# A fixed TensorE order for the scan stage of mixer groups 1 to 3, with the y products of two chunks in a row

## The chip, the cores and the metric

The kernel runs on one core of a Trainium2 chip. The metric is the device time of one execution in microseconds (us): 1355.12, the median of three runs (1355.06 to 1355.35). Five engines work side by side, each with its own in-order queue of instructions: TensorE (PE; its weight loads are shown apart as PEld), VectorE (DVE), ScalarE (ACT), GpSimd (POOL) and SyncE (SP, which here issues weight transfers). They wait for one another through semaphores.

## The reference

The reference is a two-layer decoder trunk on 512 tokens with a width of 1024. Layer 0 is a Mamba-2 mixer and a gated feed-forward block with a short convolution; layer 1 is a differential attention and the same kind of feed-forward block. The change lies in the mixer. It projects the normed input to a gate z, to x, B and C (which pass a causal convolution of width 4 and a SiLU) and to a step dt. Then it runs a chunked scan, in 4 groups of 8 heads, over chunks of 128 tokens:

```
cb       = einsum('bclgn,bcsgn->bcgls', cc, bc)
y_diag   = einsum('bcgls,bgrcls,bcsgrp->bclgrp', cb, decay_in, xc)
states   = einsum('bclgn,bgrcl,bclgrp->bcgrpn', bc, decay_states, xc)
new_states = einsum('bgrzc,bcgrpn->bzgrpn', decay_chunk, states0)
y_off    = einsum('bclgn,bcgrpn,bgrcl->bclgrp', cc, states_in, exp(a_cs))
y        = (y_diag + y_off + x * d_skip) * silu(z)
```

Then y is normed within its group and projected back, and the result is added to the residual stream.

## The kernel before

Every large product is made of three matmuls on split operands: weights high times input high, weights high times input low, weights low times input high (`mm3`, L195 to L198). One such set of three on a block of 128 of the contraction is called a triple here. A weight chunk is fetched by SyncE, its high part is copied by ScalarE (`wh`, L147), and VectorE subtracts to get the low part (`wl`, L151). `chunk()` (L187) emits these two chunks ahead of use, in the order of the list `plan`.

The mixer loops over four groups (L755). For each group the program does the following, in this order:

1. It fetches the decay masks of the four chunks through GpSimd's DMA queue (`fetch`, L618: `m`, four buffers, and `er`, two buffers).
2. It makes six convolution blocks (`conv_block`, L526): one for B (`bT`), one for C (`cT`), four for x (`xs`). Each is 24 matmuls into a `ps_in` bank, a multiplication, three shifted multiply-adds (`ctmp`, L534) and a SiLU. The norm of the group before (`normed`, L738) lies between the first two.
3. It runs the scan of the group's four chunks and the four z blocks (`z_blocks`, L710). A z block is eight triples, or 24 matmuls, into a `ps_in` bank, then a multiplication by the norm's factor (L714) and a SiLU (L715).
4. It multiplies y by z (L777), sums squares (`gsq`, `gacc`) and makes the norm's factor (`token_rsqrt`, with the transposes `tr_g`).
5. It projects the group before (`out_proj`, L698, `ps_o`). In group 3 the norm's factor and the norm are made inside the projection of group 2, and group 3's own projection follows at once.

The scan of a chunk (class `Chunk`, L606) has these steps. `tokens` (L647) transposes the chunk's x (`xs`, four transposes) and scales it by dt (`xd`, VectorE) and by the decay (`xe`, VectorE); for all but the last chunk it also transposes B (`bt` into a bank, then ScalarE copies it out, L661). `masked` (L639) multiplies C and B (`cb`, L643) and VectorE multiplies the decay mask `m` by it (L644). `states` (L663) first makes the part of y that comes from the state before (`yo`, L669, with VectorE's multiplication into `er`, L671), then the chunk's state (`st`, L674) and from it the running state `S` (ScalarE for chunk 0, two VectorE operations later). `outputs` (L682) makes the diagonal part of y: eight calls (`y`, L689), two of them side by side on the two halves of the array's columns, since each has 64 output rows; VectorE then adds the skip term and the state's part in place (L693, L696). The profile records `cb`, `yo`, `st` and `y` with two records for a call, a transpose with one.

Each of these small products takes one of four PSUM banks (`aux_bank`, L60); z and the projections take one of four others (`mm_bank`).

What sets the order: a planner takes the instructions of the program, and with its own costs and the order in which the program names them as priority, it lays out the queue of each engine before the kernel runs. Before the change the program names a step of the scan and z blocks in turn (`weave`, L470), and the planner mixes scan products and z triples on TensorE as it sees operands become ready. Some stretches are fixed by hand: inside `tc.manual_schedule` TensorE keeps the order of the program, as the attention does already (L1133).

Of the kernel before, what the change touches and what calls it, by code (L numbers as in the profile page):

```python
# [9 lines left out]
F32 = mybir.dt.float32  # L10
F32R = mybir.dt.float32r
I32 = mybir.dt.int32
AF = mybir.ActivationFunctionType
ALU = mybir.AluOpType
# [4 lines left out]
P = 128  # L19
T = 512  # L20
D = 1024
KB = D // P
NT = T // P
# [16 lines left out]
def trunk_kernel(ctx: ExitStack, tc, x, ssm_ln_g, ssm_in_w, ssm_conv_w, ssm_conv_b, ssm_dt_bias,  # L40
# [4 lines left out]
    act, dve, pool, pe, sync = nc.scalar, nc.vector, nc.gpsimd, nc.tensor, nc.sync  # L45
# [11 lines left out]
    def mm_bank(name):  # L57
        return pp.tile([P, T], F32, tag="mm", name=name)

    def aux_bank(name):  # L60
        return pp.tile([P, T], F32, tag="aux", name=name)
# [62 lines left out]
    state = {"next": 0, "use": 0}  # L124
# [62 lines left out]
    def chunk(key):  # L187
        while state["next"] <= state["use"] + AHEAD and state["next"] < len(plan):
            emit_chunk()
        state["use"] += 1  # L190
        k, h, l = ready.pop(0)
        assert k == key, (k, key)
        return h, l

    def mm3(ps, wh, wl, xh, xl, start, stop):  # L195
        pe.matmul(ps, wh, xh, start=start, stop=False)  # L196
        pe.matmul(ps, wh, xl, start=False, stop=False)  # L197
        return pe.matmul(ps, wl, xh, start=False, stop=stop).ins  # L198
# [4 lines left out]
    ident = cp.tile([P, P], F32, name="ident")  # L203
# [13 lines left out]
    xgh = [gp.tile([P, T], F32R, name="xgh%d" % k) for k in range(KB)]  # L217
    xgl = [gp.tile([P, T], F32R, name="xgl%d" % k) for k in range(KB)]
# [19 lines left out]
    with tc.tile_pool(name="ph0", bufs=1) as p0:  # L238
# [24 lines left out]
        ps = aux_bank("pst")  # L263
# [206 lines left out]
    def weave(main, fill, num, den):  # L470

        owed = 0
        for _ in main:
            owed += num
            while owed >= den:
                owed -= den
                next(fill, None)
        run(fill)
# [37 lines left out]
    with tc.tile_pool(name="ssm_y", bufs=1) as yp, tc.tile_pool(name="ssm", bufs=1) as sp:  # L516
# [89 lines left out]
        class Chunk:  # L606
# [40 lines left out]
            def tokens(self):  # L647

                tag, cs = self.tag, self.cs
                ps = aux_bank("xs" + tag)  # L650
                for b in range(4):
                    pe.transpose(ps[:, b * P:(b + 1) * P], self.xs[:, b, cs], ident)
                self.xd = sp.tile([P, HPG, 64], F32, tag="xd", name="xd" + tag, bufs=2)
                dve.tensor_tensor(out=self.xd, in0=byh(ps), in1=self.per_head(dt), op=ALU.mult)
                if self.c < NT - 1:
                    self.xe = sp.tile([P, HPG, 64], F32, tag="xe", name="xe" + tag, bufs=2)
                    dve.tensor_tensor(out=self.xe, in0=self.xd, in1=self.per_head(dl), op=ALU.mult)
                    ps = aux_bank("bt" + tag)
                    pe.transpose(ps[:, :P], self.bT[:, cs], ident)
                    self.bt = sp.tile([P, P], F32, tag="bt", name="bt" + tag, bufs=2)  # L660
                    act.activation(self.bt, ps[:, :P], AF.Copy)  # L661

            def states(self):  # L663

                tag, c = self.tag, self.c
                if c:
                    ps = aux_bank("yo" + tag)
                    for b in range(4):
                        pe.matmul(ps[:, b * P:(b + 1) * P], fl(self.prev.S[:, 2 * b:2 * b + 2, :]),  # L669
                                  self.cT[:, self.cs], start=True, stop=True)  # L670
                    dve.tensor_tensor(out=fl(self.er), in0=ps, in1=fl(self.er), op=ALU.mult)  # L671
                if c < NT - 1:
                    ps = aux_bank("st" + tag)
                    pe.matmul(ps, self.bt, fl(self.xe), start=True, stop=True)  # L674
                    self.S = sp.tile([P, HPG, 64], F32, tag="S", name="S" + tag, bufs=2)
                    if c == 0:
                        act.activation(fl(self.S), ps, AF.Copy)
                    else:
                        dve.tensor_tensor(out=self.S, in0=self.prev.S, in1=self.per_head(et), op=ALU.mult)
                        dve.tensor_tensor(out=self.S, in0=byh(ps), in1=self.S, op=ALU.add)  # L680

            def outputs(self):  # L682

                g, c, cs = self.g, self.c, self.cs
                ps = aux_bank("y" + self.tag)
                for b in range(4):
                    o = ps[:, b * P:(b + 1) * P]
                    for j in range(2):
                        pe.matmul(o[64 * j:64 * (j + 1), :], self.xd[:, 2 * b + j, :], self.m[:, 4 * j + b, :],  # L689
                                  start=True, stop=True)  # L690
                for b in range(4):
                    x_ = self.xs[:, b, cs]
                    dve.scalar_tensor_tensor(out=x_, in0=x_, scalar=c2[:, 64 + 4 * g + b:65 + 4 * g + b],  # L693
                                             in1=ps[:, b * P:(b + 1) * P], op0=ALU.mult, op1=ALU.add)
                if c:
                    dve.tensor_tensor(out=self.xs[:, :, cs], in0=self.xs[:, :, cs], in1=self.er, op=ALU.add)  # L696
# [13 lines left out]
        def z_blocks(g, zs):  # L710
            for b in range(4):
                ps = in_block("in%d" % (4 * g + b))
                z = sp.tile([P, T], F32, tag="z", name="z%d_%d" % (g, b), bufs=4)
                dve.tensor_tensor(out=z, in0=ps, in1=rr[0], op=ALU.mult)  # L714
                act.activation(z, z, AF.Silu)  # L715
                zs.append(z)
                yield

        def chunks(g, bT, cT, xs):
            cs = []  # L720
            for c in range(NT):
                cs.append(Chunk(g, c, bT, cT, xs, cs[-1] if cs else None))
            return cs

        def scan(cs):
            for t in range(NT + 1):
                if t < NT:
                    cs[t].tokens()
                    cs[t].masked()
                if t == 0:  # L730
                    cs[2].decays()
                    cs[3].decays()
                if t:
                    cs[t - 1].states()
                    cs[t - 1].outputs()
                yield

        def normed(g, xs, rt):  # L738
            with tc.issue_after(state["last"]):
# [15 lines left out]
        for g in range(NG):  # L755
            bT = sp.tile([P, T], F32, tag="bT", name="bT%d" % g, bufs=2)
            cT = sp.tile([P, T], F32, tag="cT", name="cT%d" % g, bufs=2)
            xs_ = sp.tile([P, 4, T], F32, tag="xs", name="xs%d" % g, bufs=2)
            cs = chunks(g, bT, cT, xs_)
            for c in cs:  # L760
                c.fetch()
            conv_block(16 + g, "in%d" % (32 + g), bT)
            if g:
                prev = normed(*todo)
            conv_block(20 + g, "in%d" % (36 + g), cT)
            if g == 0:
                params_a()
            xs = [xs_[:, b, :] for b in range(4)]
            for b in range(4):
                if b >= 2:  # L770
                    cs[b - 2].decays()
                conv_block(4 * g + b, "in%d" % (16 + 4 * g + b), xs[b])
            zs = []
            weave(scan(cs), z_blocks(g, zs), 2, 3)
            acc = None
            for b in range(4):
                dve.tensor_tensor(out=xs[b], in0=xs[b], in1=zs[b], op=ALU.mult)  # L777
                sq = sp.tile([P, T], F32, tag="gsq", name="gsq%d_%d" % (g, b), bufs=2)
                act.activation(sq, xs[b], AF.Square)
                if b == 0:  # L780
                    acc = sq
                else:
                    a2 = sp.tile([P, T], F32, tag="gacc", name="gacc%d_%d" % (g, b), bufs=2)
                    (pool if b == 1 else dve).tensor_tensor(out=a2, in0=acc, in1=sq, op=ALU.add)
                    acc = a2
            factor = lambda: token_rsqrt(acc, sp, "g%d" % g, 512)
            if g == 0:
                params_b()
                todo = g, xs, factor()
            elif g < NG - 1:  # L790
                run(out_proj(g - 1, *prev, None))
                todo = g, xs, factor()
            else:
                op = out_proj(g - 1, *prev, None)
                for _ in range(3):
                    next(op)
                rt = factor()
                for _ in range(2):
                    next(op)
                prev = normed(g, xs, rt)  # L800
                run(op)
# [406 lines left out]
```

## Time and profile before

| | us |
|---|---|
| median of three runs | 1355.12 |
| lowest and highest | 1355.06, 1355.35 |
| the profiled execution | 1354.9 |
| its span, first to last instruction | 1353.2 |
| scan stage of group 1, from its first transpose to the projection's first matmul | 121.42 to 156.98 |
| scan stage of group 2 | 212.33 to 247.74 |
| scan stage of group 3 | 303.09 to 338.54 |

The times of the stages are starts in the timeline, from the span's start. A record of a matmul is longer than the distance between two matmuls, since they are pipelined: a matmul of 512 columns is recorded with 0.39 us, and the next starts 0.23 us later. So distances are taken from end to end (start plus length), or from the chain of work that ended last, which counts each piece from the end of the piece before it.

### The profile page before, as it was taken

The page shows a single profiled execution, that of the slowest core. Times are in us where ns is not written, and L with a number is a line of the kernel's source. Part 1 is how long each engine was busy: PE and PEld are TensorE (multiplying, and loading weights), DVE is VectorE, ACT ScalarE, POOL GpSimd, SP SyncE. Part 2 cuts the span into 40 slices and gives each one's busy share as a digit, 9 for nine tenths or more (in the row PEclk, how much of TensorE's full clock was granted, in tenths as well). Part 3 has the DMA queues.
Part 4 walks back from the last instruction along what each step waited for, and adds up shares of the span by engine and source line. Part 5 has one row for each costly group of instructions (what it writes and reads, how often), then busy time and mean ns, then how long its engine had stood idle before and what let it go on. Part 6 is the DMA issues. An engine that isn't in the chain of part 4 may idle for free.

```text
span 1353.2 us, 16871 instructions
## 1 busy us (share of the span) xinstructions
PE 1346.1 (99%) x6417; PEld 1096.0 (81%) x6417; DVE 911.4 (67%) x1524; ACT 654.0 (48%) x1064; POOL 102.6 (8%) x142
## 2 busy tenths in 40 slices
PE   9999999999999999999999999999999999999998
PEld 7877887887888888888888877777888888888887
DVE  4989878688777774267754555778777773367742
ACT  5696844642444442234433556777654442134420
POOL 6230301200020000000001200000110000000000
PEclk9999999999999999999999999999999999999999
DMA  7452433432333333333323422221232322333322
GB/s 203 144 165 78 157 101 94 148 94 68 97 94 94 94 94 105 97 94 94 98 82 103 132 78 93 72 75 36 78 89 87 104 94 94 93 102 101 94 94 78
DMA packets 179825, 134.98 MB, mean 100 GB/s; under 512 B 6492, under 2 KB 163552, under 8 KB 179744
## 3 DMA queue, kind: packets, MB, share of 16 engines
q1 hardware_dynamic: 173872, 120.73, 29.6%
q0 software_dynamic: 4592, 12.08, 2.8%
q8 instruction: 50, 0.82, 0.2%
q10 hardware_dynamic: 1280, 1.10, 0.2%
q14 instruction: 31, 0.25, 0.1%
HBM read 131.64 MB, written 2.25 MB: 99 GB/s over the span
## 4 chain that ended last, share of the span: by engine, by line
PE 94%; DVE 3%; ACT 1%; issue 1%; DMA 0%; POOL 0%; SPq 0%; DVEq 0%; ACTq 0%
PE ps_g L197 6%; PE ps_g L196 6%; PE ps_g L198 6%; PE ps_u L196 6%; PE ps_u L197 6%; PE ps_u L198 6%; PE ps_in L197 5%; PE ps_in L196 5%; PE ps_in L198 5%; PE ps_d L851 3%; PE ps_d L196 3%; PE ps_d L852 3%; PE ps_d L197 3%; PE ps_d L853 3%; PE ps_d L198 3%; PE ps_o L198 2%
## 5 line engine op out<-in xcount | busy, mean ns | idle before, releaser
L196 PE MATMUL ps_u<-xgh,wh_u 128*128 128x512 f32 x352 | 137.4, 390 | 0.0
L197 PE MATMUL ps_g<-xgl,wh_g 128*128 128x512 f32 x352 | 137.1, 389 | 0.0
L196 PE MATMUL ps_g<-xgh,wh_g 128*128 128x512 f32 x352 | 137.0, 389 | 0.0
L198 PE MATMUL ps_u<-xgh,wl_u 128*128 128x512 f32 x352 | 137.0, 389 | 0.0
L198 PE MATMUL ps_g<-xgh,wl_g 128*128 128x512 f32 x352 | 137.0, 389 | 0.0
L197 PE MATMUL ps_u<-xgl,wh_u 128*128 128x512 f32 x352 | 136.9, 389 | 0.0
L196 PE MATMUL ps_in<-xgh,wh_in 128*128 128x512 f32 x304 | 120.9, 398 | 0.0
L197 PE MATMUL ps_in<-xgl,wh_in 128*128 128x512 f32 x304 | 120.8, 398 | 0.0
L198 PE MATMUL ps_in<-xgh,wl_in 128*128 128x512 f32 x304 | 119.5, 393 | 0.0
L151 DVE TENSOR_TENSOR wl_d<-wr_d,wh_d 128x1024 fp32r<-128x1024 f32 (+1 forms) x46 | 54.2, 1178 | 96.9 <-ACT wh_d L147 96.7
L147 ACT ACTIVATE wh_d<-wr_d 128x1024 fp32r<-128x1024 f32 (+1 forms) x46 | 47.2, 1026 | 130.5 <-PE ps_d L853 62.3
L875 ACT ACTIVATE hh<-vg 128x512 fp32r<-128x512 f32 x44 | 27.9, 634 | 115.0 <-DVE vg L874 115.0
L823 DVE TENSOR_TENSOR uu<-ps_u,nr_f 128x512 f32<-128x512 f32 x44 | 30.4, 692 | 78.0 <-PE ps_u L198 77.9
L197 PEld LDWEIGHTS ps_g<-xgl,wh_g 128*128 128x128 f32 x352 | 66.1, 188 | 13.9 <-DVE xgl L413 0.3
L198 PEld LDWEIGHTS ps_u<-xgh,wl_u 128*128 128x128 f32 x352 | 66.0, 188 | 13.9
L198 PEld LDWEIGHTS ps_g<-xgh,wl_g 128*128 128x128 f32 x352 | 66.1, 188 | 13.7
L196 PEld LDWEIGHTS ps_u<-xgh,wh_u 128*128 128x128 f32 x352 | 66.2, 188 | 13.6
L196 PEld LDWEIGHTS ps_g<-xgh,wh_g 128*128 128x128 f32 x352 | 66.0, 188 | 13.7
L197 PEld LDWEIGHTS ps_u<-xgl,wh_u 128*128 128x128 f32 x352 | 66.1, 188 | 13.4
L147 ACT ACTIVATE wh_g<-wr_g 128x1024 fp32r<-128x1024 f32 x44 | 46.8, 1063 | 51.6 <-PE ps_u L197 32.2
L196 PE MATMUL ps_d<-hh,wh_d 128*128 128x512 f32 x176 | 68.5, 389 | 0.0
L197 PE MATMUL ps_d<-hl,wh_d 128*128 128x512 f32 x176 | 68.5, 389 | 0.0
(348 smaller groups left out, 3183.8 us busy)
## 6 DMA issues: line engine op xcount, KB each, us to landing
wr_g<-in_ffn_up_w_dram SPq DMA_DIRECT2D x44, 512.0 KB, 3.7
wr_u<-in_ffn_up_w_dram SPq DMA_DIRECT2D x44, 512.0 KB, 3.7
wr_d<-in_ffn_down_w_dram SPq DMA_DIRECT2D x42, 512.0 KB, 3.6
wr_in<-in_ssm_in_w_dram SPq DMA_DIRECT2D x40, 512.0 KB, 3.8
m<-cumd POOLq DMA_DIRECT2D x16, 512.0 KB, 4.1
wr_out<-in_ssm_out_w_dram SPq DMA_DIRECT2D x16, 512.0 KB, 3.4
wr_k<-in_kv_w_dram SPq DMA_DIRECT2D x8, 512.0 KB, 3.7
wr_q<-in_q_w_dram SPq DMA_DIRECT2D x8, 512.0 KB, 3.7
```

The lines of the kernel that those rows point to most:

```text
L147: return act.activation(self.wh[:, :self.n], self.raw[:, :self.n], AF.Copy)
L151: return eng.tensor_tensor(out=self.wl[:, :self.n], in0=self.raw[:, :self.n], in1=self.wh[:, :self.n].bitcast(F32), op=ALU.subtract)
L196: pe.matmul(ps, wh, xh, start=start, stop=False)
L197: pe.matmul(ps, wh, xl, start=False, stop=False)
L198: return pe.matmul(ps, wl, xh, start=False, stop=stop).ins
L823: dve.tensor_tensor(out=u, in0=ps, in1=r, op=ALU.mult)
L851: pe.matmul(pss[b], hh[k][:, ts], wh[:, k - k0, :], start=k == 0, stop=False)
L852: pe.matmul(pss[b], hh[k][:, ts], wl[:, k - k0, :], start=False, stop=False)
L853: pe.matmul(pss[b], hl[k][:, ts], wh[:, k - k0, :], start=False, stop=k == n - 1)
L875: act.activation(h, ga, AF.Copy)
```

## The change

The steps of a chunk are cut finer. B's transpose leaves `tokens` and becomes `turned`; `states` loses its first half, which becomes `preceding` (the part of y from the state before); `outputs` loses its matmuls, which become `products`. Group 0 calls them in the old order and stays woven by the planner.

For groups 1 to 3 a new function `woven` names the order. It goes through the 32 z triples of a group, one at a time, and behind certain triples it does certain steps; TensorE keeps this order. The number is that of the triple, from 0; in group 1 all steps come five triples later (`behind`). Chunks are a, b, c and d.

```
-            weave(scan(cs), z_blocks(g, zs), 2, 3)
+            if g:
+                woven(cs, g, zs)
+            else:
+                weave(scan(cs), z_blocks(g, zs), 2, 3)
...
+        def z_steps(g, zs):
+            for b in range(4):
+                wh, wl = chunk("in%d" % (4 * g + b))
+                ps = mm_bank("ps_in%d" % (4 * g + b))
+                for k in range(KB):
+                    state["last"] = mm3(ps, wh[:, k, :], wl[:, k, :], xgh[k], xgl[k], k == 0, k == KB - 1)
+                    if k == KB - 1:
+                        z = sp.tile([P, T], F32, tag="z", name="z%d_%d" % (g, b), bufs=4)
+                        dve.tensor_tensor(out=z, in0=ps, in1=rr[0], op=ALU.mult)
+                        act.activation(z, z, AF.Silu)
+                        zs.append(z)
+                    yield
...
+        def woven(cs, g, zs):
+
+            def pair(a, b):
+                a.products()
+                b.products()
+                a.outputs()
+                b.outputs()
+
+            a, b, c, d = cs
+            at = {0: (a.turned, b.turned, c.decays), 1: (a.masked, b.masked, d.decays),
+                  10: (a.tokens,), 11: (b.tokens,), 13: (a.states,), 15: (b.preceding, b.states),
+                  16: (lambda: pair(a, b), c.turned, c.masked), 18: (c.tokens,), 19: (c.preceding, d.tokens),
+                  20: (d.masked,), 21: (c.states,), 24: (d.preceding,), 25: (lambda: pair(c, d),)}
+            with tc.manual_schedule(engines={mybir.EngineType.PE}):
+                behind = 5 if g == 1 else 0
+                for n, _ in enumerate(z_steps(g, zs)):
+                    for f in at.get(n - behind, ()):
+                        f()
```

So the `y` matmuls of chunks a and b follow one another behind triple 16, and those of c and d behind triple 25; the transposes of B of chunks a and b come first of all, behind triple 0, and their `cb` products behind triple 1. The matmuls, transposes, copies and transfers are the same in number and shape as before. VectorE, ScalarE, GpSimd and SyncE are still laid out by the planner.

More of the change, by code (lines that the diff above doesn't have):

```diff
@@ L657, in tokens, with turned, preceding @@
                     dve.tensor_tensor(out=self.xe, in0=self.xd, in1=self.per_head(dl), op=ALU.mult)
[L658 to L663, printed above, removed]
+            def turned(self):
+                tag = self.tag
+                ps = aux_bank("bt" + tag)
+                pe.transpose(ps[:, :P], self.bT[:, self.cs], ident)
+                self.bt = sp.tile([P, P], F32, tag="bt", name="bt" + tag, bufs=2)
+                act.activation(self.bt, ps[:, :P], AF.Copy)
+            def preceding(self):
                 tag, c = self.tag, self.c
@@ L671, in states @@
                     dve.tensor_tensor(out=fl(self.er), in0=ps, in1=fl(self.er), op=ALU.mult)
+            def states(self):
+                tag, c = self.tag, self.c
                 if c < NT - 1:
@@ L680, in states, with products @@
                         dve.tensor_tensor(out=self.S, in0=byh(ps), in1=self.S, op=ALU.add)
-            def outputs(self):
-                g, c, cs = self.g, self.c, self.cs
-                ps = aux_bank("y" + self.tag)
+            def products(self):
+                ps = self.y = aux_bank("y" + self.tag)
                 for b in range(4):
@@ L690, in outputs @@
                                   start=True, stop=True)
+            def outputs(self):
+                g, c, cs = self.g, self.c, self.cs
+                ps = self.y
                 for b in range(4):
@@ L728, in scan @@
                     cs[t].tokens()
+                    if t < NT - 1:
+                        cs[t].turned()
                     cs[t].masked()
@@ L733, in scan @@
                 if t:
+                    cs[t - 1].preceding()
                     cs[t - 1].states()
+                    cs[t - 1].products()
                     cs[t - 1].outputs()
                 yield
+        def woven(cs, g, zs):
[14 more added lines that the diff above has]
+                        f()
         def normed(g, xs, rt):
```

## The prediction

> **What bounds the kernel now.** The page first: span, engines, chain.
>
> ```profile
> span 1353.2 us, 16871 instructions
> PE 1346.1 (99%) x6417; PEld 1096.0 (81%) x6417; DVE 911.4 (67%) x1524; ACT 654.0 (48%) x1064; POOL 102.6 (8%) x142
> PE 94%; DVE 3%; ACT 1%; issue 1%; DMA 0%; POOL 0%; SPq 0%; DVEq 0%; ACTq 0%
> ```
>
> TensorE is busy for 99% of the span and carries 94% of the chain that ended last. So an edit can only win where TensorE spends time without doing work inside what the page calls busy, and it loses as soon as TensorE waits. The change touches the scan stage of groups 1 to 3: from the end of the last convolution block's matmuls to the first matmul of the output projection. The view by windows, one window for each such stage, comes second:
>
> ```profile
> 121.40:157.00 35.60, 35.60 (x219) 27.69 (x218) 33.56 (x55) 22.68 (x44) 7.91 (x12) 1.00 0.47 154
> 212.30:247.70 35.40, 35.40 (x218) 27.77 (x217) 29.15 (x49) 19.57 (x40) 9.67 (x14) 1.00 0.38 122
> 303.10:338.50 35.40, 35.40 (x218) 27.77 (x217) 30.21 (x51) 9.53 (x16) 2.33 (x3) 1.00 0.21 67
> ```
>
> Columns are length, then PE, PEld, DVE, ACT and POOL busy, the granted clock, the DMA share and GB/s. TensorE is full in all three, VectorE is the next engine (33.56 of 35.60 in group 1, 29 to 30 later), the clock is at 1.00. The three stages have the same work and nearly the same length. Busy time hides where TensorE loses, because matmuls overlap in the records. The chain view counts each piece from the end of the one before it, so it comes third, for group 2 (start, length, what):
>
> ```profile
> 222.50 0.86 PE st L674 x2
> 223.35 1.02 PE y L689 x16
> 224.38 0.59 PE xs L652 x4
> ...
> 225.53 1.07 PE yo L669 x8
> ...
> 227.46 1.02 PE y L689 x16
> 228.49 0.43 PE ps_in L197
> 228.91 0.23 PE ps_in L198
> ...
> 231.21 0.44 PE xs L652 x4
> 231.87 0.89 PE yo L669 x8
> ...
> 233.62 1.02 PE y L689 x16
> 234.65 0.43 PE ps_in L196
> ...
> 238.26 1.02 PE y L689 x16
> 239.29 0.43 PE ps_in L198
> ```
>
> Three things are to be seen. A `ps_in` matmul takes 0.23 us, but the one right behind a `y` run takes 0.43: **0.20 lost at the exit** of each run, three times. Four `xs` transposes take 0.44, but 0.59 behind a `y` run: 0.15 lost. And the `yo` run of 225.53 takes 1.07 where the next takes 0.89: 0.18 lost. What a `y` run costs to enter is seen in the timeline, cut inside the first run:
>
> ```profile
> 223.28 0.33 PE L689 MATMUL y<-m,xd 128*64 128x128 f32 x2
> 223.28 0.44 PE L689 MATMUL y<-m,xd 128*64 128x128 f32 x4
> ```
>
> Two more records, one pair on the two column halves, add 0.11. Eight pairs make 0.88, the run takes 1.02, so **some 0.15 is lost at the entry** of each of the four runs (0.14 by the rounded rows; I take 0.15, the size seen at the exit to `xs`).
>
> The other losses stand in the timeline and in the waits:
>
> ```profile
> 203.03 0.39 PE L197 MATMUL ps_in<-xgl,wh_in 128*128 128x512 f32 x1
> ...
> 212.10 0.39 PE L198 MATMUL ps_in<-xgh,wl_in 128*128 128x512 f32 x1
> ...
> 213.23 0.47 PE L196 MATMUL ps_in<-xgh,wh_in 128*128 128x512 f32 x1
> 213.57 0.33 PE L659 MATMUL bt<-ident,bT 128*128 128x128 f32 x1
> ...
> 214.20 0.40 PE L196 MATMUL ps_in<-xgh,wh_in 128*128 128x512 f32 x1
> 214.44 0.49 PE L643 MATMUL cb<-cT,bT 128*128 128x128 f32 x2
> ...
> 219.70 0.48 PE L197 MATMUL ps_in<-xgl,wh_in 128*128 128x512 f32 x1
> ...
> 222.10 0.39 PE L198 MATMUL ps_in<-xgh,wl_in 128*128 128x512 f32 x1
> ```
> ```profile
> PEld cb L643 <- ACT bt L661: 0.3, 1, 0.3
> PEld yo L669 <- ACT bt L661: 0.2, 1, 0.2
> PEld bt L659 <- ACT bt L661: 0.2, 1, 0.2
> ```
>
> Undisturbed, 40 steps from 203.03 to 212.10 take 9.07, so 0.227 each and **0.68 for a z triple**. End against end, `bt` takes 213.90 - 213.70 = 0.20, where a transpose takes 0.11 (0.44 / 4): 0.09 lost. `cb` takes 214.93 - 214.60 = 0.33, where two passes of `yo`'s size take 0.22 (0.89 / 4): 0.11 lost. The waits name the cause of these two and of the late `yo`: each wants a PSUM bank that ScalarE's copy of a transposed B still holds. Last, the ten z matmuls from 219.70 to 222.10 end 2.31 after the first, not 2.27: a break in the z stream costs some 0.03 beyond the rest.
>
> **The change part by part**, for one group.
>
> *Two y runs in a row.* Four runs become two. Two entries go: 2 x 0.15 = 0.30. Exits were 0.15 + 3 x 0.20 = 0.75. Afterwards the first pair is followed by chunk 2's `bt`, a transpose like `xs` (0.15), and the second by a z triple (0.20): 0.35, so 0.40 is saved. What lies between two `y` runs in a row is not in the trace: no run follows another. Bounds: 0, as between the pairs inside a run, and 0.15, as at an entry. I take 0, because the second run has the same shape on the same column halves as the pairs inside the first. The Trainium skill, TensorEngine Tiling (Array Packing), section Tiling Modes, says that a change of the tiling mode drains TensorE and a change of the tile alone does not; the 0.15 and 0.20 above agree, by that rule the second run pays nothing, and the sum stays.
>
> *B's transposes first.* `bt` and `cb` of chunks 0 and 1 go behind z triples 1 and 2: four tiles for four banks that nothing else holds by then. Chunk 2's follow the first pair, where they want the banks of `yo` (step 15) and `st`, let go by one and two VectorE operations, with 1.9 of `y` matmuls in between. So the three waits go: 0.09 + 0.11 + 0.18 = 0.38. If VectorE is late there, the cover is gone and the same banks make a new wait (a rival, below).
>
> *The fixed order.* The extra work now enters the z stream at 13 steps and not at 8 places, so five more breaks at up to 0.03, fewer where a step has no fill between: -0.09 taken, between 0 and -0.15. Nothing else is added: the matmuls, transposes, copies and DMAs are the same in number and shape.
>
> Sum for a group: 0.30 + 0.40 + 0.38 - 0.09 = **0.99**. Three groups, taken alike: **3.0**. Group 0 keeps its weave.
>
> *What hides the moved steps.* VectorE and ScalarE first, by these rows:
>
> ```profile
> 129.76 0.63 ACT L536 ACTIVATE xs<-ctmp 128x512 f32<-128x512 f32 x1 [0.45 <-DVE ctmp L534]
> 218.75 0.63 ACT L536 ACTIVATE xs<-ctmp 128x512 f32<-128x512 f32 x1 [4.37 <-DVE ctmp L534]
> 220.14 1.28 DVE L654 TENSOR_TENSOR xd<-xs,dt 128x512 f32<-128x512 f32 x2
> 222.54 1.22 DVE L151 TENSOR_TENSOR wl_in<-wr_in,wh_in 128x1024 fp32r<-128x1024 f32 x1
> 226.27 1.21 DVE L644 TENSOR_TENSOR m<-m,cb 128x1024 f32<-128x1024 f32 x1
> ```
>
> Step 10 (`xs` of chunk 0) needs the last convolution block's output. It comes 11 triples (7.48), two `bt` (0.22) and two `cb` (0.45) into the stage, at 8.2. In group 2 that output was there at 219.38, 7.1 after the stage began; in group 1 at 130.39, 9.0 after. So group 1 without the shift would wait 0.8; five triples later it is 11.6 and has 2.6 to spare. From there VectorE needs about 0.6 for a 512-wide operation (two in 1.28) and 1.2 for a 1024-wide one. `st` of chunk 0 (step 13) comes 2.5 after `xs`'s transposes; xd and xe take 1.2, a weight split ahead of them 1.2 more: just enough. The pair at step 16 needs masks whose products were formed at step 1, some 14 earlier. From step 21's `st` to step 24's `yo` lie 2.0; two S operations take 1.2. All steps hold if VectorE takes this work when it is ready.
>
> The last pair ends six triples before the stage does (one in group 1), later than the last `y` did, so the outputs, the gate products and the norm sums move later. Groups 1 and 2 have the whole output projection of the group before as cover. Group 3 has least:
>
> ```profile
> 342.85 0.69 DVE L784 TENSOR_TENSOR gacc<-gacc,gsq 128x512 f32<-128x512 f32 x1
> ```
> ```profile
> 346.87 0.44 PE tr_g L445 x4
> ```
> The timeline first, then the chain: the sum was ready at 343.54 and first used at 346.87: 3.3 of cover. Eight outputs and two adds are about 3.4 of VectorE, the last pair leaves 4.1 to the stage's end, and the last z block, which the sum also needs, isn't later. So nothing; past 3.3 every us would count in full, since `al_g` and the last projection follow.
>
> DMAs: the y runs let go of the m tiles, so GpSimd's queue fetches the next group's masks some us later; they are first used in the next scan. Chunk 3's er fetch stands in that same queue behind them:
>
> ```profile
> DVE er L671 <- DMA er<-cumd: 1.3, 1, 1.3
> ```
> In group 2 VectorE already waits 1.3 for it. It may wait longer, with chunk outputs and z products queued behind it, but TensorE needs none of these before the projection's fourth block. Nothing. SyncE's weight fetches stay triggered by the same z blocks.
>
> The profiled execution is 1354.9 (span 1353.2): 1354.9 - 3.0 = 1351.9. The median, 1355.12, lies 0.2 above it: **1352.1**.
>
> **The rivals.**
>
> *Slower: TensorE waits for VectorE inside the fixed order.* Its place is step 24, where `yo` wants chunk 2's S, and step 13, where `st` wants xe. Before, z matmuls filled such gaps; now a late operand holds all of them behind it. If the planner queues a mask product (1.2), a z product (0.6) and a weight split (1.2) ahead of the two S operations, S comes 4.2 after `st`, against 2.0: a wait of 2.2. At step 13 likewise up to 1.0. That is 3.2 a group, 9.6 less 3.0: +6.6, **1361.7**. Below 1.0 a group it only eats the gain; it decides from 1.9 a group. For it: VectorE is busy 33.56 of 35.60 in group 1, and its queue is in order. Against: 5 to 6 us of slack in groups 2 and 3, and the shift in group 1. The Trainium skill, PSUM — Partial Sum Buffer, section Engine vs sequencer instructions, says that matmuls start and complete in program order; `yo` at 225.53, with ready z matmuls behind it and 0.18 lost, agrees.
>
> *The second run of a pair pays an entry after all* (0.15, six times): 0.9 less, **1353.0**. Against it: 0.11 a pair inside a run.
>
> *New short waits take the place of the old:* the three bank waits return at steps 16 and 18 to 20, or VectorE is late by half a us once or twice a group: 0.6 a group, 1.8 less, **1353.9**. For it: before, too, each bank wait was a copy only just late.
>
> **How the numbers follow.** 0.2% (2.7 us, about what a measurement of this kernel can tell from no change) sets the bound at 1352.4, just above the forecast. Forecast 0.57, with a range of its own from 1351.5 (`yo` and exits a little better) to 1352.8 (breaks at 0.03 everywhere, entries 0.14): three quarters of it under the bound. Second entry 0.12, short waits 0.15: both within 0.2%. Slower 0.16. So faster 0.44, same 0.40, slower 0.16. The range reaches over the two middle cases, 1351.5 to 1355.5, and leaves out the slower one and some of the edges.
>
> **What would show it.** The chain of the new trace has `y` runs of 32 records in about 1.9, one 0.43 behind them a group and no 1.07 for `yo`; each stage is 34.4 to 34.6 long. A second run of 1.02 speaks for the second entry. `yo`, `st` or `cb` in the waits of PEld on VectorE, with chain pieces over 1 us at steps 13 or 24, speak for the slower case. A gap ahead of `tr_g` or the last projection in group 3 would mean that the cover there was too thin.

## The result and the profile after

| | before | after |
|---|---|---|
| median, us (13 runs of each) | 1355.12 | 1352.54 |
| lowest to highest | 1354.14 to 1357.32 | 1351.55 to 1354.45 |
| profiled execution | 1354.9 | 1352.86 |
| its span | 1353.2 | 1351.1 |

The ratio is 0.9983, with a 95% interval from 0.9976 to 0.9990. The medians lie 2.6 us apart, the two profiled executions 2.0; the forecast was 3.0. By the interval the gain is between 1.4 and 3.3, so the medians alone can't tell 3.0 from 2.0, and what follows is read from marks inside the profiled executions. The page of after (span, engines, chain by engine):

```profile
span 1351.1 us, 16873 instructions
PE 1343.6 (99%) x6417; PEld 1096.6 (81%) x6417; DVE 913.7 (68%) x1524; ACT 647.8 (48%) x1060; POOL 106.2 (8%) x142
PE 93%; DVE 3%; ACT 2%; issue 1%; DMA 0%; POOL 0%; SPq 0%; DVEq 0%; ACTq 0%
```

TensorE still bounds the kernel, with as many matmuls as before (x6417). Beyond the span and 2.5 us less of TensorE's busy time the page doesn't tell the two kernels apart. To see where the 2.0 came from, the run is cut at marks that both kernels have: the first `tr_g` transpose of each group, and the feed-forward's first `ps_g` matmul behind the mixer. The timeline of TensorE, in before:

```profile
100.70 0.66 PE L445 MATMUL tr_g<-ident,gacc 128*128 128x128 f32 x4
178.75 0.60 PE L445 MATMUL tr_g<-ident,gacc 128*128 128x128 f32 x4
269.51 0.60 PE L445 MATMUL tr_g<-ident,gacc 128*128 128x128 f32 x4
346.71 0.60 PE L445 MATMUL tr_g<-ident,gacc 128*128 128x128 f32 x4
383.00 0.39 PE L196 MATMUL ps_g<-xgh,wh_g 128*128 128x512 f32 x1
```

and in after:

```profile
100.70 0.66 PE L445 MATMUL tr_g<-ident,gacc 128*128 128x128 f32 x4
178.14 0.60 PE L445 MATMUL tr_g<-ident,gacc 128*128 128x128 f32 x4
268.47 0.60 PE L445 MATMUL tr_g<-ident,gacc 128*128 128x128 f32 x4
344.69 0.60 PE L445 MATMUL tr_g<-ident,gacc 128*128 128x128 f32 x4
381.00 0.39 PE L196 MATMUL ps_g<-xgh,wh_g 128*128 128x512 f32 x1
```

The distances between marks are the groups' times. Group 0 is 100.70 in both. Group 1 went from 78.05 to 77.44, group 2 from 90.76 to 90.33, group 3 from 77.20 to 76.22; the tail of the mixer, 36.29 and 36.31, and all behind it are the same within 0.04. So the gains are 0.6, 0.4 and 1.0. (The experiments below use the same marks to three digits: 0.60, 0.44, 0.97.) Only group 3 got what was forecast for each. The windows of the scan stages of groups 2 and 3, cut from the first z matmul to the projection's first, columns as before, say the same:

```profile
211.74:246.70 34.96, 34.70 (x218) 27.80 (x217) 31.13 (x50) 17.60 (x33) 7.48 (x12) 1.00 0.44 126
302.07:336.52 34.45, 34.45 (x218) 27.89 (x217) 30.36 (x50) 8.85 (x14) 1.04 (x2) 1.00 0.23 69
```

In group 3 TensorE is busy for all of the 34.45, and the forecast for each stage was 34.4 to 34.6. In group 2 the stage is 0.51 longer and 0.26 of it is idle. GpSimd's column differs: 12 instructions in group 2, two in group 3. First the chain of group 3, where all went well:

```profile
318.09 1.90 PE y L696 x32
319.99 0.26 PE bt L663
...
321.87 0.44 PE xs L652 x4
...
323.00 0.89 PE yo L673 x8
...
330.48 1.90 PE y L696 x32
332.37 0.43 PE ps_in L196
332.80 0.23 PE ps_in L197
```

A run of 32 `y` records takes 1.90: sixteen pairs of 0.11 and one entry of 0.14, so the second chunk's run pays no entry. `bt` behind it takes 0.26, 0.15 more than a transpose; the one `ps_in` behind a run takes 0.43; no `xs` takes 0.59 and no `yo` 1.07. Now the waits of after inside the scan stage of group 1 (the row is word for word the same in group 2; group 3 has none):

```profile
PE st L682 <- DVE xe L657: 0.3, 1, 0.3
```

One `st` in each of these two groups waited for VectorE's xe. In group 1 it is that of step 13. VectorE's timeline there, then the chain:

```profile
133.21 0.69 DVE L739 TENSOR_TENSOR z<-ps_in,nr_x 128x512 f32<-128x512 f32 x1 [0.68 <-PE ps_in L198]
133.82 0.68 DVE L654 TENSOR_TENSOR xd<-xs,dt 128x512 f32<-128x512 f32 x1
134.42 1.22 DVE L151 TENSOR_TENSOR wl_out<-wr_out,wh_out 128x1024 fp32r<-128x1024 f32 x1
135.55 0.69 DVE L657 TENSOR_TENSOR xe<-xd,dec 128x512 f32<-128x512 f32 x1
```
```profile
136.38 1.10 PE st L682 x2
```

The planner put a weight split (`wl_out`, 1.22) between chunk 0's xd and xe, and a z product ahead of xd. xe is done at 136.24, `st` starts at 136.38 and takes 1.10 on the chain where an undisturbed one takes 0.86. The wait of 0.25 (0.3 in the rounded row) and the 0.24 make 0.49. In group 2 it is the `st` of step 21, with another cause. The timeline of GpSimd and VectorE, and the same operation of the same chunk in group 3 as the last row:

```profile
234.10 1.09 POOL L632 TENSOR_SCALAR_AFFINE_SELECT m<-m 128x1024 f32<-128x1024 f32 x1 [3.59 <-DMA m<-cumd]
234.29 1.45 DVE L657 TENSOR_TENSOR xe<-xd,dec 128x512 f32<-128x512 f32 x1
...
324.61 0.68 DVE L657 TENSOR_TENSOR xe<-xd,dec 128x512 f32<-128x512 f32 x1
```

Nothing stood ahead of xe in the queue that was not there in group 3, but it took 1.45 instead of 0.68. It had begun while GpSimd was at work on the next group's decay mask (the selection of L632). Group 3 has no next group and no selection. The `st` at 235.88 again lost 0.50.

### The profile page after: what moved, and what is told of

Same layout as the page of the kernel before. It is cut to its first block, busy times and chain, and to the rows that moved or that the text cites. A ratio compares the mean times of both kernels' runs of the same rounds, so it can differ in the third digit from the quotient of the medians.

```text
span 1351.1 us, 16873 instructions
## 1 busy us (share of the span) xinstructions
PE 1343.6 (99%) x6417; PEld 1096.6 (81%) x6417; DVE 913.7 (68%) x1524; ACT 647.8 (48%) x1060; POOL 106.2 (8%) x142
## 4 chain that ended last, share of the span: by engine, by line
PE 93%; DVE 3%; ACT 2%; issue 1%; DMA 0%; POOL 0%; SPq 0%; DVEq 0%; ACTq 0%
PE ps_g L197 6%; PE ps_g L198 6%; PE ps_g L196 6%; PE ps_u L198 6%; PE ps_u L196 6%; PE ps_u L197 6%; PE ps_in L196 4%; PE ps_in L197 4%; PE ps_in L198 4%; PE ps_d L902 3%; PE ps_d L198 3%; PE ps_d L197 3%; PE ps_d L904 3%; PE ps_d L903 3%; PE ps_d L196 3%; PE ps_o L198 2%
## 5 line engine op out<-in xcount | busy, mean ns | idle before, releaser
L196 PE MATMUL ps_in<-xgh,wh_in 128*128 128x512 f32 x304 | 126.2, 415 | 0.0
```

## The experiments

**Theory:** the sum is right (entries, exits, bank waits), and what is missing is two waits of TensorE for xe, one from the order of VectorE's queue in group 1, one from GpSimd's mask selection in group 2. **Rival A:** the saving is smaller than the sum and the waits are incidental. **Rival B:** one of the parts (B first, the fixed order, the shift) earns nothing or costs. The edits are to the kernel after. "Group gain" is the distance of marks in before less that in the run, for groups 1, 2, 3; after has 0.60, 0.44, 0.97.

### The y runs of a pair apart

```
-                  16: (lambda: pair(a, b), c.turned, c.masked), ...
+                  16: (lambda: (a.products(), a.outputs()), c.turned, c.masked),
+                  17: (lambda: (b.products(), b.outputs()),), ...
-                  ... 25: (lambda: pair(c, d),)}
+                  ... 25: (lambda: (c.products(), c.outputs()),),
+                  26: (lambda: (d.products(), d.outputs()),)}
```

> The changed kernel's fixed order, but the two y runs of a pair stand apart: a's behind triple 16, b's behind 17, c's behind 25, d's behind 26. All else stays. Theory (a ledger: each entry into a y run costs 0.15 us on TensorE, each exit 0.15 to a transpose and 0.20 to a z matmul, a second run directly behind the first costs nothing, and every such item goes one for one into the time): two more entries and two more exits to z a group, 0.70, and two more breaks of the z stream at 0.02 to 0.03; +0.75 a group, +2.2 us on the changed kernel in all, the mixer's end (first matmul of the feed-forward part) 2.2 later, and y records in runs of 16 with 1.02 each in the chain. Rival (the gain comes from the fixed order and from the three bank waits that went, not from the pairing): within 0.5 us of the changed kernel.

Measured: 1354.88 beside 1354.91 for before, ratio 1.0000 (0.9990 to 1.0009). Groups 1 and 3 are 0.74 and 0.75 longer than in after. Group 2 is only 0.25 longer: its xe wait of 0.50 did not occur in this execution, and with that put aside it is 0.75 too. Together that is the 2.2 of the theory. The chain of group 3:

```profile
332.18 1.02 PE y L696 x16
333.21 0.43 PE ps_in L196
...
334.10 1.02 PE y L696 x16
335.12 0.43 PE ps_in L196
```

Each run pays its entry and its exit again. So the rows that priced the pairing give its price, 0.7 a group. Without it the rest of the change gives 0.19 and 0.22 in groups 2 and 3, and -0.13 in group 1, where step 13's wait is still there.

### The pairing alone

The scan is woven with the z blocks by the planner, as in before, but the products of two chunks are named together.

```
+                    elif t % 2 == 0:
+                        cs[t - 2].products()
+                        cs[t - 1].products()
+                        cs[t - 2].outputs()
+                        cs[t - 1].outputs()
...
-                woven(cs, g, zs)
+            weave(scan(cs), z_blocks(g, zs), 2, 3)
```

> The pairing alone: the planner weaves scan steps and z blocks as it did before, B's transposes stay with the tokens, but in groups 1 to 3 the y products of chunks 0 and 1, and of 2 and 3, are named one after the other. Ledger: two entries (0.30) and 0.40 of exits a group are saved against the kernel before, the three bank waits on ScalarE's copies (0.38 to 0.43 a group) stay; -0.7 a group, -2.1 us against before, so within 0.5 of the changed kernel, whose two waits for VectorE (0.49 each) are not expected here. Rival (the fixed order and B's transposes first make the gain): at most 0.5 us faster than before. Second rival (the planner's order gives new waits on VectorE when the outputs come in pairs): slower than the ledger by the waits that the trace then shows.

Measured: 1352.88, ratio 0.9986 (0.9976 to 0.9995); group gains 0.67, 0.59, 0.60, so 1.86. Its chain and its waits in group 2:

```profile
237.76 1.90 PE y L696 x32
239.66 0.43 PE ps_in L197
```
```profile
PEld cb L643 <- ACT bt L665: 0.3, 1, 0.3
...
PEld yo L673 <- DVE S L688: 0.2, 1, 0.2
PEld bt L663 <- ACT bt L665: 0.2, 1, 0.2
```

The runs are paired, and waits for banks (ScalarE's copy of `bt`) and for S remain. No xe wait is there. So the pairing by itself gives 1.86 of the 2.02 that the change brought with its two waits. The fixed order adds 0.4 in group 3, where nothing is late, and lost 0.07 and 0.15 in groups 1 and 2 of after.

### B's transposes beside their chunk's tokens

```
-            at = {0: (a.turned, b.turned, c.decays), 1: (a.masked, b.masked, d.decays),
-                  10: (a.tokens,), 11: (b.tokens,), ...
+            at = {0: (c.decays,), 1: (d.decays,),
+                  10: (a.tokens, a.turned, a.masked), 11: (b.tokens, b.turned, b.masked), ...
```

Chunk c's go from step 16 to 18 in the same way.

> The fixed order and the pairing as in the changed kernel, but B's transposes and the products of B and C are not first: each stands directly behind its own chunk's x transposes (triples 10, 11 and 18). Ledger: the bank waits come back in part, 0.1 to 0.5 us a group, as the transposes of chunk 1 find banks still held, and two breaks of the z stream go (-0.05); +0.2 to +1.4 us on the changed kernel in all. Rival (putting B first earned nothing, since VectorE's mask products are what TensorE would wait for): above +2 us, with waits of the y products on the masks in the trace. Third possibility: within 0.2 us, so that B's transposes first are of no use by themselves.

Measured: 1352.87, ratio 0.9982 (0.9973 to 0.9991). Group 3 is 0.02 shorter than in after, and no wait for a bank came back in any group, where the ledger had 0.1 to 0.5. Group 2 is 0.53 shorter, since its xe wait did not occur. Group 1 is 0.72 longer: step 13's wait is gone, and a new one of `yo` at step 24 has come. VectorE, GpSimd and the chain there:

```profile
148.26 2.73 DVE L151 TENSOR_TENSOR wl_out<-wr_out,wh_out 128x1024 fp32r<-128x1024 f32 x1
```
```profile
148.80 1.11 POOL L632 TENSOR_SCALAR_AFFINE_SELECT m<-m 128x1024 f32<-128x1024 f32 x1
```
```profile
153.97 1.16 PE yo L673 x8
```

A split that takes 1.22 elsewhere took 2.73 beside a selection, and S stood behind it in the queue. So "B first" earns nothing by itself, as rival B has it for this part: in group 3 the other place did as well under the fixed order. And the wait for S, which the prediction feared at step 24, exists: the split's 1.51 extra is more than the 0.81 by which S was late. (The selection alone doesn't account for all of it: the split began 0.54 ahead of it and lost more than its 1.11. What held the split before that stays open.)

### No shift in group 1

```
-                behind = 5 if g == 1 else 0
+                behind = 0
```

> The changed kernel without the five triples in group 1. Ledger: in group 1 the x transposes of chunk 0 wait for the last convolution block, whose output came 9.0 us into the stage while step 10 comes at 8.2: 0.8 us, and the states behind it then wait for xe with VectorE still busy, 0.2 to 1.5 more; +1.0 to +2.3 us on the changed kernel, less the wait of 0.49 at step 13 that the changed kernel has there. Groups 2 and 3 as in the changed kernel. Rival (the shift is not needed, or costs by piling up the end of group 1): within 0.3 us or faster.

Measured: 1354.30, ratio 0.9994 (0.9985 to 1.0003). Group 1 is 1.48 longer than in after. Its waits:

```profile
PE st L682 <- DVE xe L657: 1.2, 1, 1.2
PE xs L652 <- ACT xs L536: 0.3, 1, 0.3
```

Both parts that the shift was credited with are there: `xs` late from the convolution (0.56 on the chain, where the prediction had 0.8), and `st` behind the queue that forms meanwhile (1.41). A shift is needed; that it must be five is not shown, and a shorter one comes below. Group 2, untouched by the edit, was without its wait this time (89.82), as in the first and third experiments.

### After once more

The kernel is not edited; one more profiled execution shows which wait recurs.

> The changed kernel once more, unchanged, for a second look at its two waits. If the wait of 0.49 for xe at step 13 of group 1 comes from the order of VectorE's queue (a weight split between xd and xe), it stands there again, 0.4 to 0.6. If the wait of 0.50 at step 21 of group 2 comes from GpSimd's mask selection happening to run over xe (a transfer's landing decides), it may be there or not: there if the selection begins up to 0.7 before xe or with it, gone otherwise, group 2 then 0.5 shorter. Rival (both are a fixed cost of the order): both again at 0.49 and 0.50.

Measured: 1352.85; group gains 0.06, 0.95, 0.97. Step 13's wait is there again (0.46). Group 2's is gone, and in group 1 another has come, at step 21. GpSimd and VectorE in group 1, then GpSimd in group 2:

```profile
148.61 1.68 DVE L657 TENSOR_TENSOR xe<-xd,dec 128x512 f32<-128x512 f32 x1
148.64 1.11 POOL L632 TENSOR_SCALAR_AFFINE_SELECT m<-m 128x1024 f32<-128x1024 f32 x1
...
234.96 1.54 POOL L632 TENSOR_SCALAR_AFFINE_SELECT m<-m 128x1024 f32<-128x1024 f32 x1 [3.86 <-DMA m<-cumd]
```

In group 1 xe and a selection began together, within 0.03, and xe took 1.68. In group 2 xe began 0.09 ahead of the selection, as VectorE's row has it:

```profile
234.87 0.68 DVE L657 TENSOR_TENSOR xe<-xd,dec 128x512 f32<-128x512 f32 x1
```

It kept its 0.68, and the selection took 1.54 instead of 1.09. So step 13's wait belongs to the order of the queue, and the other to chance: it depends on when a mask's transfer lands. Of the six profiled executions with the fixed order and early masks (after three times, and the first, third and fourth experiments) one has it in group 2 and one in group 1.

### The next group's masks later

```
-                pool.dma_start(self.m, cumd[0][i].partition_broadcast(P))
+                d = pool.dma_start(self.m, cumd[0][i].partition_broadcast(P))
+                if self.c == 0 and self.g >= 2:
+                    pin(d)
```

`pin` keeps an instruction behind those that the program names before it on its engine. So the masks of groups 2 and 3 are fetched behind the scan.

> The changed kernel, but GpSimd's fetch of the first mask of groups 2 and 3 is held behind everything GpSimd was given before it, so the masks of the next group are fetched and selected after the group's norm sums and no longer during the scan. Theory (exclusive use: VectorE's xe took 1.45 in place of 0.68 because GpSimd's selection was running): no VectorE operation of the scan in groups 1 and 2 over 1.3 but the 1024-wide ones, the wait at step 21 of group 2 gone, group 2 as long as group 3's like part, 0.95 to 1.0 under before; the wait at step 13 of group 1 stays. Rival (xe is late by its place in the queue): the wait at step 21 stays at 0.4 to 0.5.

Measured, in one execution: 1351.93; group gains 0.56, 0.95, 0.97. GpSimd's selections for group 2, first and last of four, now lie behind group 1's scan, and the view of the tile xe gives least, middle and greatest duration (ns) of the nine calls in the three groups:

```profile
168.71 1.09 POOL L634 TENSOR_SCALAR_AFFINE_SELECT m<-m 128x1024 f32<-128x1024 f32 x1 [1.68 <-DMA m<-cumd]
...
174.79 1.68 POOL L634 TENSOR_SCALAR_AFFINE_SELECT m<-m 128x1024 f32<-128x1024 f32 x1 [0.35 <-DMA m<-cumd]
```
```profile
L659 DVE TENSOR_TENSOR xe<-xd,dec x9: 677/691/692, 135.2 to 323.7; 128x512 f32<-128x512 f32 x9
```

No xe is stretched, group 2 has no wait, and step 13's wait in group 1 stays (0.46). That group 2 has no wait would prove little by itself, since most executions had none there; but now no selection runs during the scans of groups 1 to 3, in this run and in the three below with the same edit, and every xe of theirs takes 0.68 or 0.69. The meetings go on behind the scan, where splits take 1.68 and 2.12 and TensorE doesn't wait for them. The two causes are apart.

### Late masks and a shift of four

```
-                behind = 5 if g == 1 else 0
+                behind = 4 if g == 1 else 0
```

This goes on top of the late masks.

> As the run before, and group 1 begins four triples later in place of five, so that xd and xe of chunk 0 are queued ahead of the weight split that a z block's end lets loose. Theory: both waits gone, -1.0 us on the changed kernel's profiled execution: the mixer's end 3.0 before that of the kernel before, the time 3.0 under it (ratio 0.9978). Rival (VectorE is full in group 1, and the wait moves on to the next step): group 1 gains less than 0.2 and another wait for VectorE or the last convolution block shows up there.

Measured: 1352.18 beside 1355.24 for before, ratio 0.9978 (0.9968 to 0.9987). Group gains 1.12, 0.95, 0.97: 3.04. Step 13 in VectorE's timeline and in the chain:

```profile
134.89 0.68 DVE L659 TENSOR_TENSOR xe<-xd,dec 128x512 f32<-128x512 f32 x1
135.49 0.69 DVE L656 TENSOR_TENSOR xd<-xs,dt 128x512 f32<-128x512 f32 x1
136.09 1.21 DVE L151 TENSOR_TENSOR wl_out<-wr_out,wh_out 128x1024 fp32r<-128x1024 f32 x1
```
```profile
136.07 0.86 PE st L684 x2
```

The split now stands behind xe, and `st` takes 0.86. With both waits gone, the three groups give the forecast's 3.0, which refutes rival A. (Group 0, the same code in all kernels, took 101.33 in this profiled execution and 100.29 to 101.08 in the others; the profiled sums of whole kernels scatter with it, the groups' own gains do not.)

### Thirteen stops merged to seven

```
+            at = {1: (a.turned, b.turned, a.masked, b.masked, c.decays, d.decays), 11: (a.tokens, b.tokens),
+                  14: (a.states,), 16: (b.preceding, b.states, lambda: pair(a, b), c.turned, c.masked),
+                  19: (c.tokens, c.preceding, d.tokens, d.masked), 22: (c.states,),
+                  25: (d.preceding, lambda: pair(c, d))}
...
+                behind = 3 if g == 1 else 0
```

With the late masks as well. It was run twice, the second time beside the kernel after on one chip.

> As the run before, with the 13 steps brought together to 7: B's transposes and both products of B and C behind triple 1, both chunks' x transposes behind 11, the first state behind 14, the next with the first pair behind 16, c's and d's x transposes with yo and cb behind 19, c's state behind 22, yo with the second pair behind 25; group 1 three triples later. Theory: six breaks of the z stream fewer at 0.02 to 0.035, -0.12 to -0.2 a group, -0.4 to -0.6 us on the run before: 3.4 to 3.6 under the kernel before (ratio 0.9974), if no new wait comes. Rival (operands that are fetched together come too late together, and four banks are too few): new waits at the states or at cb of 0.3 to 1 us a group, and the time is that of the changed kernel or above.

> The kernel after once more, timed beside the next one on one chip. By its groups' marks it stands 2.0 to 2.6 below before, so 0.9981 to 0.9985 of it, and where group 2's wait happens not to occur 0.5 lower. Group 1 keeps the wait of st at step 13, 0.4 to 0.5 long, since it lies in the order of VectorE's queue.

> The version with late masks and seven merged stops, timed beside the kernel after. If the two waits are all that after loses, it stands 1.0 to 1.2 below after in the mixer's groups 1 to 3 (3.2 against 2.0 to 2.5 below before), 0.9 to 1.2 in the medians. The rival, that its lower median on the other chip was scatter of group 0, expects a difference under 0.5 in the medians.

Measured, first: 1351.88, ratio to before 0.9975 (0.9966 to 0.9984). Then, side by side: after 1352.67 (1351.77 to 1353.35), ratio 0.9984 (0.9975 to 0.9993); merged 1351.61 (1351.24 to 1352.04), ratio 0.9977 (0.9968 to 0.9986). The version with neither wait is 1.06 faster than after in the medians, inside the 0.9 to 1.2 expected, and the rival's scatter of under 0.5 is out. In their profiled executions the gap is 0.62 at the end of the mixer, since after's group 2 was without its wait (group gains 0.61, 0.95, 0.97); where the rest of the 1.06 comes from, no trace shows. Merging by itself gave 0.03 to 0.05 a group over the kernel with 13 stops, far less than the 0.12 to 0.2 expected (0.04 in groups 2 and 3; group 1 also has another shift). This version has the lowest median of all that ran.

A run of all four chunks' `y` in a row was not tried: chunk d's er takes the buffer of chunk b's, which b's outputs let go only behind b's products.

## Why the prediction was right, and where it was not

The median, 1352.54, lies 0.4 above the forecast of 1352.1, just above 1352.4, where the prediction drew its bound between faster and same, and inside both of its ranges. The gain forecast for a group came in group 3 alone.

**Entries and exits: right, term by term.** Two entries of 0.15 and 0.40 of exits were forecast. The runs of 32 take 1.90, `bt` behind one 0.26, z behind the other 0.43, and taking the pairs apart costs 0.74. The prediction's open point, what lies between two runs in a row, is settled at nothing. The Trainium skill, TensorEngine Tiling (Array Packing), section Tiling Modes, says that a change of the tiling mode drains TensorE and a change of the tile alone doesn't. The 1.90 instead of 2.04 agrees.

**Bank waits: right in size, not in cause.** No `bt`, `cb` or `yo` of after waits for ScalarE's copy of B. But their removal is the work of the fixed order as such: with B's transposes back beside the tokens these waits stayed away, and group 3 was no slower.

**Breaks: too dear.** Five more were taken at 0.09 a group. Six fewer stops gave 0.04 in groups 2 and 3, so under 0.01 each, inside the range given. In sum, group 3 gave 0.97 where 0.99 was worked out.

**The shift in group 1: right that one is needed, not in its size.** Without it `xs` and `st` wait, and the group is 1.48 longer. But with five, step 13 fell behind the split; with four it didn't.

**The step that failed** is in the part on what hides the moved steps: "All steps hold if VectorE takes this work when it is ready". It doesn't, for two reasons. At step 13 the prediction had counted xd, xe and one weight split, 2.4 in all, against 2.5 between the transposes and `st`, and called this "just enough". The work was as counted, 2.42 from the start of xd to the end of xe, with the split in the middle. What the sum left out lies around it. xd began 0.21 behind the transposes' end (133.61), since a z product stood ahead of it; in group 3 it began 0.04 behind. `st` began 0.14 behind xe. And without the wait `st` would have begun at 135.96, 0.23 behind the last z matmul. So 2.77 was needed where 2.35 was there, and `st` cost 0.46 to 0.49 more in each of the three profiled executions of after.

The second reason is the masks. Their DMAs were put down as "Nothing", as if the masks were first used in the next scan. The fetches were followed to the transfer, but not to GpSimd's selection, which runs when the mask lands, still in this scan, and lengthens VectorE's work. That cost 0.50 in group 2 of the profiled execution, as much in group 1 of another, and nothing in a third. 3.0 - 0.49 - 0.50 is 2.0, the gap of the two profiled executions. The gaps of the medians, 2.6 and in the second comparison 2.1, lie between 2.0 and the 2.5 that one wait leaves, or close to that; how often the second wait occurs in them is not shown, so that the median came no further from the forecast is in part luck.

**The rivals.** The slower one named the right mechanism and one of the right places, step 13, at half of the 1.0 it could have cost there; at step 24 S was in time in after and late by 0.8 only in an experiment. It decides from 1.9 a group, and no group of after lost more than 1.0 to such waits (0.46 and 0.52 in group 1 of the second profiled execution). The third, VectorE late by half a us once or twice a group, came true in part: 1.0 in all instead of 1.8. The second entry does not exist (1.90 for a run of 32). So the time lies between the forecast (1351.9 for the profiled execution) and the third rival (1353.7 on that scale), at 1352.86.

**Covers that held.** In group 3 the norm's sum was the thinnest:

```profile
341.37 1.47 DVE L835 TENSOR_TENSOR gacc<-gacc,gsq 128x512 f32<-128x512 f32 x2
```

It ends at 342.84, 1.85 before `tr_g` at 344.69. Of the cover of 3.3 some 1.5 was used up, and the last projection did not move.

## What to carry to other kernels

Small products that need another tiling of the array belong side by side: here the price was paid per run, and it could be read off the first matmul behind a run before anything was changed. An order fixed by hand turns each late operand into a wait of the whole engine, where a planner can slip other work in. So each fixed step needs more slack than the sum of its own operations: room for what else the queue may put in front, and for the hand-overs. Here 0.1 was left by that sum, and `st` was late. And a transfer that moves must be followed to the operation that uses what it brings, since that one may take another engine's time.

## What the runs showed of the hardware

In these traces a VectorE operation whose two inputs both lie in SBUF and a selection of GpSimd hold each other up. xe took 1.45 and 1.68 beside one, 0.93 where it met only the end of one (fourth experiment), and 0.68 or 0.69 in all its other calls in groups 1 to 3; the split took 2.73 instead of 1.22. Where xe began 0.09 ahead, it was the selection that took 1.54 instead of 1.09; 0.03 ahead was not enough. xd, with one input in PSUM, kept its 0.68 when it began 0.11 into a selection of after (146.67 to 147.76). The Trainium skill, GPSIMD Engine Reference, section Specifications, lists GpSimd's SBUF interfaces as shared with VectorE, with contention when a VectorE instruction has two SBUF inputs; these numbers agree. Before had such meetings too, with the first S operation (0.68 or 0.69 in the other groups' calls) beside a selection:

```profile
145.22 1.08 POOL L632 TENSOR_SCALAR_AFFINE_SELECT m<-m 128x1024 f32<-128x1024 f32 x1 [3.09 <-DMA m<-cumd]
145.37 1.48 DVE L679 TENSOR_TENSOR S<-S,dec 128x512 f32<-128x512 f32 x1
```

TensorE didn't wait for this S; in the planner's weave other matmuls stood in between. The rule stood against the "Nothing" of the prediction and was not used there.

A wait costs TensorE more than its length in the waits view. `st` takes 1.10 on the chain behind a wait and 0.86 without, and the 0.24 is the same behind a wait of 0.25 and one of 1.2 (fourth experiment). In the timeline the record of `st` grows only from 1.02 to 1.10; the other 0.16 is the overlap with the matmul ahead, which ends 0.16 behind the start of an undisturbed `st` (136.07 and 135.91 in group 1 of the late masks with a shift of four) and which is lost when TensorE has run empty.
